# Dilated attention on Trainium2: the two key blocks of dilation 1 folded into one tile of scores

## The chip, the cores and the metric

The kernel runs on one core of one Trainium2 chip. Its time is the device time of one launch in microseconds, and the median of several runs is compared. The engines have the names of the profile: PE (TensorE matmuls), PEld (its weight loads), DVE (VectorE), ACT (ScalarE), POOL (GpSimd) and SP (SyncE, which here only issues DMAs).

## The reference

The kernel computes one step of a hybrid decoder layer: in every layer, an HGRN2 recurrence and a dilated sliding-window attention run beside each other on a prompt of 2048 positions and on eight sample requests, followed by an output projection, a ConvFFN and a per-layer input gate. Only the prompt's attention is touched here. It has 8 heads of 64 channels and three dilations, whose partial results are merged by their maxima and sums:

```python
DILATIONS = ((128, 1), (512, 4), (2048, 16))      # window, dilation
dist = qi - kj + ATTN_BLOCK                       # qi: 128 queries, kj: 256 keys (previous block, own block)
for window, dil in DILATIONS:
    n_back = window // dil                        # 128 for each
    ...
    valid = (dist >= 0) & (dist <= n_back) & (blk * ATTN_BLOCK - ATTN_BLOCK + kj >= 0)
    s = jnp.einsum('brnqhc,brnkhc->brnhqk', qs, kb)
    s = jnp.where(valid[None, None, :, None], s, NEG_INF)
    m = s.max(axis=-1)
    p = jnp.exp(s - m[..., None])
    l = p.sum(axis=-1)
    acc = jnp.einsum('brnhqk,brnkhc->brnqhc', p, vb)
    parts.append((from_sub(m), from_sub(l), from_sub(acc)))
w = jnp.exp(ms - ms.max(axis=0, keepdims=True))   # combine_dilations
return (w[..., None] * accs).sum(0) / (w * ls).sum(0)[..., None]
```

In dilation 1 each query reads 129 keys: its own position and the 128 before it. In a block of 128 queries, a query at place i of the block reads own keys at places 0 to i and the previous block's keys at places i to 127. So at each place there is exactly one key that counts, own or previous, except at place i itself, where both count (distances 0 and 128).

## The kernel before

**Stages.** The first stage, up to about 837 us, holds the input projection and most of the HGRN2 recurrence. The attention stage follows, to about 1213 us, and then the trunk (output projection, ConvFFN, gate), whose matmuls fill PE to the end. In the attention stage the prompt's attention is interleaved with side work: the last unit of the recurrence, the attention of the samples (its keys and values arrive as 32 DMAs of 1 MB into tiles `skt`), and the samples' recurrence.

**Order.** On PE the order of instructions is the order of a table set by hand. On DVE, ACT and POOL a scheduler places them by an estimate of when their inputs come. The DMAs of this stage are issued mostly by SP, in the order of its queue.

**Blocks and units.** Heads are taken in four pairs, p = 0 to 3. A pair has two kinds of blocks of 128 queries. With `di == 0`, dilations 4 and 16 are done together: the queries are every fourth position of a chunk of 512, the keys all positions of their residue up to the chunk's end (1 to 4 tiles of 128 keys), and a key that both dilations read counts twice, by adding log 2 to its score. With `di == 1`, dilation 1, there are 16 blocks with two key blocks each, the previous and the own one (the first block only has its own). A unit is one block with both heads, or with one head where it has 3 or 4 key tiles. There are 160 units: 40 to a head pair, the last 16 of them dilation 1 for pairs 0 to 2. In pair 3 both kinds alternate.

**Steps.** Step x of the loop `for x in range(n + 19)` issues, for unit x, `scores`: four matmuls into a bank `S` of PSUM (keys split in a high part `kH` and a low part `kL`, L797 and L798), a DVE instruction for each head that adds the mask, writes the result `P` to SBUF and takes the minimum (L802; scores are held negated), and ACT's exponential with its sum (L803). At odd x, two older units (x-3 and x-2) are `turned`: PE transposes `P` into a bank `PT` (L810), and the result is copied to SBUF as `pt`, for three of four units by DVE and for the fourth by ACT (L812). Then the units x-7 and x-6 are summed: `weighted` multiplies `pt` with the values into a bank `acc` (L822). Four blocks, a group, share one `acc`; after the fourth, ACT copies it to SBUF as `o` (L872). There are 32 groups.

**Merge and staging.** After each dilation-1 group `merge` (L728 to L761) combines it with the same queries' other group: statistics go out and come back by DMA, DVE and POOL make the weights, ACT one exponential, and coefficients go out and come back. For the next head pair, `stage` loads queries and keys by DMA, and `stack` writes them to `qS`, `kH` and `kL` (L695 is ACT's part), in four pieces around the end of the pair before.

**Banks.** In PSUM, `S`, `acc` and `PT` have two banks each; the rest is for the side work.

Of the kernel before, what the change touches and what calls it, by code (L numbers as in the profile page):

```python
# [28 lines left out]
BIG = 1e30  # L29
# [18 lines left out]
def hymba_step_kernel(ctx: ExitStack, tc: tile.TileContext, I: dict, O: dict):  # L48
# [624 lines left out]
    def attn_phase(spare, rest):  # L673
# [29 lines left out]
        qS = rp.tile([128, 2, SEQ], F32R, name="qS")  # L703
        kH = rp.tile([128, 2, 4, 512], F32R, name="kH")
        kL = rp.tile([128, 2, 4, 512], F32R, name="kL")
        mask = wk.tile([128, 768], F32, name="mask", bufs=1)
        SP.dma_start(mask, I["amask"])
        stack(0, *first)
        yield
        vals = {}  # L710
# [52 lines left out]
        class Block:  # L763


            def __init__(self, p, di, c, r):
                self.p, self.di, self.c, self.r = p, di, c, r
                self.pt = {}
                if di == 0:
                    self.q = lambda hh: qS[:, hh, 512 * c + r:512 * c + 512:4]  # L770
                    self.nk = c + 1
                    self.k = lambda t, hh: t[:, hh, r, :128 * c + 128]
                    self.v = [(n, r) for n in range(c + 1)]
                else:
                    b = 4 * c + r
                    self.q = lambda hh: qS[:, hh, 128 * b:128 * b + 128]
                    self.nk = 2 if b else 1
                    self.k = lambda t, hh: t[:, hh].rearrange("p r (n i) -> p n r i", i=32)[:, b + 1 - self.nk:b + 1]
                    self.v = [(x // 4, x % 4) for x in range(b + 1 - self.nk, b + 1)]
                hi = (512, 768)[di]  # L780
                self.mask = mask[:, hi - 128 * self.nk:hi]

        class Unit:
# [5 lines left out]
            def scores(self, both):  # L789
                bl = self.block  # L790
                bl.both, bl.st = both, both[:, 1]
                st = bl.st
                w = 128 * bl.nk
                s = pS.tile([128, 512], F32, name="S")
                self.pe = wk.tile([128, 512], F32, name="P", bufs=6)
                for i, hh in enumerate(self.heads):
                    PE.matmul(s[:, w * i:w * i + w], lhsT=bl.q(hh), rhs=bl.k(kH, hh), start=True, stop=False)  # L797
                    PE.matmul(s[:, w * i:w * i + w], lhsT=bl.q(hh), rhs=bl.k(kL, hh), start=False, stop=True)  # L798
                for i, hh in enumerate(self.heads):
                    pe = self.pe[:, w * i:w * i + w]  # L800
                    mn = st[:, bl.r, hh, 1:2]
                    V.tensor_tensor_reduce(pe, s[:, w * i:w * i + w], bl.mask, 1.0, 3e38, ALU.add, ALU.min, mn)  # L802
                    A.activation(pe, pe, AF.Exp, bias=mn, scale=-1.0, accum_out=st[:, bl.r, hh, 0:1])  # L803

            def turned(self, on_act):
                nk = self.block.nk
                n = nk * len(self.heads)
                pt = pT.tile([128, 4, 128], F32, name="PT")
                for i in range(n):
                    PE.transpose(pt[:, i], self.pe[:, 128 * i:128 * i + 128], ident)  # L810
                out = wk.tile([128, 4, 128], F32, name="pt", bufs=8)
                (A.copy if on_act else V.tensor_copy)(out[:, :n], pt[:, :n])  # L812
                for i, hh in enumerate(self.heads):
                    self.block.pt[hh] = out[:, nk * i:nk * i + nk]
# [790 lines left out]
    for x in in_phase(1, *args, plv, po):  # L1605
# [5 lines left out]
        else:  # L1611
# [3 lines left out]
    pool = pools(attn_st)  # L1615
    pps = pool("s_ps", 1, space=PSUM)
    rest += (pool("a_d", 2), pool("a_r", 1), pool("a_w", 3), pool("a_s", 3),
             pool("a_pS", 2, space=PSUM), pool("a_pA", 2, space=PSUM), pool("a_pT", 2, space=PSUM))
    step(main, 1)

    def others():
# [43 lines left out]
def _constants():  # L1665

    f = np.float32
    c = {}
    c["ident"] = np.eye(128, dtype=f)
    inv = (500000.0 ** (-np.arange(8) * 0.125)).astype(f)  # L1670
    pos = np.zeros((17, 128), f)
    pos[:16] = np.arange(SEQ, dtype=f).reshape(16, 128)
    pos[16, :NS] = (16384 + np.arange(NS) % 4).astype(f)
    ang = (pos[:, :, None] * inv).astype(np.float64)
    cos, sin = np.cos(ang).astype(f), np.sin(ang).astype(f)
    c["rope"] = np.ascontiguousarray(np.concatenate([cos, cos, -sin, sin], -1).transpose(1, 0, 2))
    i = np.arange(128)


    dist = i[:, None] - i[None, :] + 128 * np.arange(3, -1, -1)[:, None, None]  # L1680
    count = ((dist >= 0) & (dist <= 128)) + ((dist >= 0) & (dist % 4 == 0)).astype(int)
    order = 4 * (i % 32) + i // 32
    keep = np.stack([order[None, :] >= i[:, None], order[None, :] <= i[:, None]]).astype(int)
    count = np.concatenate([count, keep]).transpose(1, 0, 2).reshape(128, 768)
    c["amask"] = np.where(count == 0, BIG, np.where(count == 2, -np.log(2.0), 0.0)).astype(f)
    m = np.zeros((128, 9, 2, 64), f)
    for li, h in enumerate(LEVELS):
        for a, n in enumerate((h, 2 * h, 2 * h)):
            right = i[(i // n) % 2 == 1]
            part = ((i[:, None] // (2 * n)) == (right[None, :] // (2 * n))) & ((i[:, None] // n) % 2 == 0)  # L1690
            if a:
                part &= (i[:, None] // h) % 2 == 2 - a
            m[:, 3 * li + a] = part[:, None]
    m = m.reshape(128, 9, 128)
    c["lvl_mask"] = m
    j = np.arange(NS)
    m = np.zeros((NS, 2, NS), f)
    for li, h in enumerate((2, 1)):
        m[:, li] = (((j[:, None] // (2 * h)) == (j[None, :] // (2 * h))) & ((j[:, None] // h) % 2 == 0)
                    & ((j[None, :] // h) % 2 == 1))  # L1700
    c["lvl_mask_s"] = m
    c["bmask"] = (j[:, None] // 4 == np.arange(8)[None, :]).astype(f)

    t = np.arange(128) % 4
    w = (np.arange(128)[None, :] * 4 + np.arange(4)[:, None]).reshape(-1)
    dist = 512 + t[:, None] - w[None, :]
    mw = (dist <= 128).astype(f) + ((dist % 4 == 0) & (dist <= 512)).astype(f)
    md = (np.repeat(np.arange(4), 128)[None, :] == t[:, None]).astype(f)
    mult = np.concatenate([mw, md], 1)
    logs = lambda n: np.where(n > 0, -np.log(np.maximum(n, 1.0, dtype=np.float64)), BIG).astype(f)  # L1710
    c["s_neg"] = logs(mult)
    mn = np.zeros((128, 2, NS), f)
    for g in range(2):
        for r in range(128):
            b, tt = 4 * g + r // 32, r % 4
            mn[r, g, 4 * b:4 * b + tt] = 1.0
            mn[r, g, 4 * b + tt] = 3.0
    c["s_negn"] = logs(mn)
    head = (np.arange(128) % 32) // 4
    c["s_hmask"] = (head[:, None] == np.arange(512)[None, :] // 64).astype(f)  # L1720
    bt = (np.arange(128) // 32) * 4 + t
    c["s_sel"] = (bt[:, None] == np.arange(16)[None, :]).astype(f)
    return c
# [75 lines left out]
```

## Time and profile before

| what | value |
|---|---|
| median of 3 runs | 3017.25 us (3016.31 to 3018.32) |
| the profiled execution's own time | 3014.84 us |
| its span in the profile | 3013.0 us |
| mean granted clock of PE | 0.988 of full speed |
| instructions in the profile | 52001 |
| bytes moved by DMA | 664.08 MB, 220 GB/s in the mean |

The span is the time from the first to the last recorded instruction; the run's time is 1.8 us longer. In rows of windows, each engine has its busy microseconds and the count of its instructions, followed by the clock that PE was granted, the share of time in which the 16 DMA engines were busy in the mean (it can read above 1), and GB/s. In rows of groups, the part behind the bar is busy time and the mean of one in ns, then the idle time of the engine ahead of them and what ended it. In rows of the chain, the first number is the place in the span and the second the share of the chain that the step takes. A row of the timeline has start, duration, engine, line and operation, and in square brackets the idle time ahead with what ended it; matmuls overlap in the pipeline, so the time from start to start tells how fast they go.

### The profile page before, as it was taken

The numbers are of one execution on the slowest core, as the hardware profiler recorded it, in microseconds if no ns is written. First come the engines' busy times: TensorE is split into PE (matmuls) and PEld (weight loads), VectorE is DVE, ScalarE is ACT, GpSimd is POOL, SyncE is SP. The second block draws the span as 40 slices with busy tenths as digits, with TensorE's granted clock in tenths as the row PEclk, the third lists the DMA queues.
The fourth block names the chain that finished last, engine by engine and source line by source line (L and its number), as shares of the span: only waits on it lengthen the run. The fifth ranks groups of instructions, "written<-read, shape, count | busy, mean of one in ns | idle before, by whom it ended". The sixth has DMA issues, their size and how long they took to land.

```text
span 3013.0 us, 52001 instructions
## 1 busy us (share of the span) xinstructions
PE 2926.5 (97%) x18639; PEld 2738.0 (91%) x18639; DVE 2191.6 (73%) x4761; ACT 1304.5 (43%) x2824; POOL 667.9 (22%) x780
## 2 busy tenths in 40 slices
PE   8999999999978989999999999999999999999998
PEld 8977789987767667999999999999999999999997
DVE  7666868884466557568988889766769777777777
ACT  5333423231156665334444444544444544444443
POOL 1443222221134553102443431000001000000000
PEclk9999999999989999999999999999999999999999
DMA  5898533342248996766666568677778777778873
GB/s 174 311 337 309 198 103 110 104 134 95 91 115 243 303 246 194 260 225 222 227 209 194 191 198 300 231 250 252 245 231 311 242 245 244 257 248 290 272 274 131
DMA packets 328579, 664.08 MB, mean 220 GB/s; under 512 B 46400, under 2 KB 114112, under 8 KB 326528
## 3 DMA queue, kind: packets, MB, share of 16 engines
q1 hardware_dynamic: 291472, 472.65, 48.4%
q0 software_dynamic: 33264, 121.13, 12.6%
q10 hardware_dynamic: 3584, 66.98, 6.1%
q8 instruction: 147, 2.41, 0.3%
q14 instruction: 112, 0.92, 0.1%
HBM read 513.69 MB, written 213.92 MB: 241 GB/s over the span
## 4 chain that ended last, share of the span: by engine, by line
PE 72%; issue 9%; DVE 7%; DMA 7%; ACT 2%; POOL 2%; SPq 1%; DVEq 0%; POOLq 0%; ACTq 0%
PE mm L142 16%; PE mm L144 16%; PE mm L143 16%; PE mm L346 2%; PE mm L344 2%; PE mm L345 2%; PE lv L484 2%; PE acc L822 2%; PE S L797 1%; PE PT L810 1%; PE S L798 1%; DMA draw<-in_w_down_dram 1%; DMA xr<-in_xT_dram 1%; DVE h L1291 1%; DMA wd_d<-dw 1%
## 5 line engine op out<-in xcount | busy, mean ns | idle before, releaser
L143 PE MATMUL mm<-w 128*128 128x348 f32 (+3 forms) x3636 | 1166.1, 321 | 1.1 <-DVE w L1435 0.7
L142 PE MATMUL mm<-w 128*128 128x348 f32 (+3 forms) x3508 | 1109.7, 323 | 15.2 <-ACT s L1233 5.8
L144 PE MATMUL mm<-w 128*128 128x348 f32 (+3 forms) x3508 | 1117.4, 321 | 1.3 <-DVE w L181 1.3
L143 PEld LDWEIGHTS mm<-w 128*128 128x128 f32 x3636 | 684.3, 188 | 3.8 <-DVE w L1067 1.8
L142 PEld LDWEIGHTS mm<-w 128*128 128x128 f32 x3508 | 656.5, 188 | 23.6 <-ACT s L1233 8.5
L144 PEld LDWEIGHTS mm<-w 128*128 128x128 f32 x3508 | 659.0, 188 | 2.6 <-DVE w L181 1.8
L181 DVE TENSOR_TENSOR w<-raw,w 128x512 fp32r<-128x512 f32 x586 | 421.9, 725 | 170.3 <-ACT w L180 165.3
L180 ACT CAST w<-raw 128x512 fp32r<-128x512 f32 x586 | 360.6, 621 | 402.8 <-PE mm L144 293.1
L1275 POOL DMA_DIRECT2D w<-wd_d x231 | 123.8, 536 | 906.2 <-PE mm L144 800.6
L1291 DVE TENSOR_TENSOR h<-h,mm 128x348 f32<-128x348 f32 (+1 forms) x504 | 248.4, 509 | 45.9 <-PE mm L144 44.4
L803 ACT ACTIVATE P<-P,st 128x256 f32<-128x256 f32 (+3 forms) x256 | 134.1, 526 | 87.5 <-DVE st L802 85.9
L802 DVE CUSTOM_DVE_ANT_0 P<-S,mask 128x256 f32<-128x256 f32 (+3 forms) x256 | 105.0, 449 | 73.1 <-PE S L798 50.1
L1233 ACT COPY s<-mm 128x348 f32<-128x348 f32 (+1 forms) x198 | 87.9, 444 | 158.1 <-PE mm L144 157.8
L345 PE MATMUL mm<-wl,xh 128*128 128x512 f32 x352 | 140.7, 400 | 1.1 <-DVE wl L267 1.1
L344 PE MATMUL mm<-wh,xh 128*128 128x512 f32 x352 | 140.6, 403 | 0.0
L346 PE MATMUL mm<-wh,xl 128*128 128x512 f32 x352 | 140.3, 399 | 0.0
L142 PE MATMUL mm<-xh,wh 128*128 128x384 f32 (+2 forms) x384 | 125.7, 332 | 8.6 <-ACT xh L242 5.1
L143 PE MATMUL mm<-xl,wh 128*128 128x384 f32 (+2 forms) x384 | 126.9, 333 | 0.8 <-DVE xl L243 0.8
L144 PE MATMUL mm<-xh,wl 128*128 128x384 f32 (+2 forms) x384 | 125.5, 330 | 1.5 <-DVE wl L267 1.4
L267 DVE TENSOR_TENSOR wl<-wraw,wh 128x512 fp32r<-128x512 f32 x104 | 86.3, 851 | 34.0 <-POOL wh L148 28.9
L181 DVE TENSOR_TENSOR dw<-draw,dw 128x512 fp32r<-128x512 f32 x77 | 69.4, 909 | 55.8 <-ACT dw L180 55.0
L797 PE MATMUL S<-kH,qS 128*128 128x256 f32 (+3 forms) x256 | 97.7, 396 | 8.2 <-DVE st L802 7.3
(348 smaller groups left out, 5155.0 us busy)
## 6 DMA issues: line engine op xcount, KB each, us to landing
w<-wd_d POOLq DMA_DIRECT2D x231, 512.0 KB, 5.6
wd_d<-dw SPq DMA_DIRECT2D x77, 512.0 KB
out_sk_dram<-in_cache_k_dram ACTq DMA_DIRECT2D x56, 584.0 KB
out_sv_dram<-in_cache_v_dram ACTq DMA_DIRECT2D x56, 584.0 KB
raw<-in_w_gate_dram SPq DMA_DIRECT2D x110, 256.0 KB
raw<-in_w_up_dram SPq DMA_DIRECT2D x110, 256.0 KB
wraw<-in_w_in_dram SPq DMA_DIRECT2D x104, 256.0 KB
raw<-w_gate_d SPq DMA_DIRECT2D x88, 256.0 KB
```

The source lines that it names most:

```text
L142: PE.matmul(ps, lhsT=wh, rhs=xh, start=first, stop=False, skip_group_check=read)
L143: PE.matmul(ps, lhsT=wh, rhs=xl, start=False, stop=False, skip_group_check=read)
L144: PE.matmul(ps, lhsT=wl, rhs=xh, start=False, stop=last, skip_group_check=read)
L180: A.copy(w[:, 0], raw)
L181: V.tensor_sub(w[:, 1], raw, f32(w[:, 0]))
L344: PE.matmul(ps, lhsT=xh[k][:, js], rhs=wh, start=k == 0, stop=False)
L345: PE.matmul(ps, lhsT=xh[k][:, js], rhs=wl, start=False, stop=False)
L346: PE.matmul(ps, lhsT=xl[k][:, js], rhs=wh, start=False, stop=k == NK - 1)
L797: PE.matmul(s[:, w * i:w * i + w], lhsT=bl.q(hh), rhs=bl.k(kH, hh), start=True, stop=False)
L803: A.activation(pe, pe, AF.Exp, bias=mn, scale=-1.0, accum_out=st[:, bl.r, hh, 0:1])
L1275: G.dma_start(t, wd_d[p][n - 1])
L1291: V.tensor_add(o, o, acc[m][:, :H])
```

## The change

In every dilation-1 block with two key blocks, 60 of the 64, the two tiles of scores are folded into one. A predicated copy on DVE, with a 0/1 mask `ahead`, writes the previous block's scores over the own block's at the places whose own key is ahead of the query, in PSUM. What remains is one tile of 128 columns for each head in place of 256: one DVE minimum over both heads, exponentials of 128 columns straight out of PSUM, and one transpose for each head in place of two. The sums still need the probabilities as two tiles, one for each key block. So in place of the copy of the transposed tiles to SBUF, DVE multiplies each of the two transposed tiles by two 0/1 masks (`sides`), one for the previous and one for the own block, and writes four tiles. All 60 products are on DVE; before, a quarter of the copies was on ACT.

The key at distance 128, whose place now belongs to the own block, moves to the blocks of `di == 0` (it is read there as the key 32 steps back in the residue), where its count rises by one, so log 3 appears beside log 2 in the mask. The mask grows from 768 to 1024 columns, and one DVE instruction casts `ahead` to bytes. The first block of each pair is not folded. The banks of PSUM are given out anew: `S` gets three, `acc` one, `PT` keeps two.

```diff
-        mask = wk.tile([128, 768], F32, name="mask", bufs=1)
+        mask = wk.tile([128, 1024], F32, name="mask", bufs=1)
         SP.dma_start(mask, I["amask"])
+        ahead = wk.tile([128, 128], U8, name="ahead", bufs=1)
+        V.tensor_copy(ahead, mask[:, 640:768])
+        sides = mask[:, 768:].rearrange("p (o n t) -> p o n t", o=1, n=2).to_broadcast([128, 2, 2, 128])
...
-                hi = (512, 768)[di]
+                self.folded = di == 1 and self.nk == 2
+                hi = (512, 640)[di]
...
+                if bl.folded:
+                    two = s.rearrange("p (h n t) -> p h n t", h=2, n=2)
+                    V.copy_predicated(two[:, :, 1], ahead.rearrange("p (o t) -> p o t", o=1).to_broadcast([128, 2, 128]),
+                                      two[:, :, 0])
+                    V.tensor_reduce(st[:, bl.r, :, 1], two[:, :, 1], axis=mybir.AxisListType.X, op=ALU.min)
+                    for hh in range(2):
+                        A.activation(self.pe[:, 128 * hh:128 * hh + 128], two[:, hh, 1], AF.Exp,
+                                     bias=st[:, bl.r, hh, 1:2], scale=-1.0, accum_out=st[:, bl.r, hh, 0:1])
+                    return
...
+                if self.block.folded:
+                    pt = pT.tile([128, 4, 128], F32, name="PT")
+                    for hh in range(2):
+                        PE.transpose(pt[:, hh], self.pe[:, 128 * hh:128 * hh + 128], ident)
+                    out = wk.tile([128, 4, 128], F32, name="pt", bufs=8)
+                    V.tensor_mul(out.rearrange("p (h n) t -> p h n t", h=2),
+                                 pt[:, :2].rearrange("p h (o t) -> p h o t", o=1).to_broadcast([128, 2, 2, 128]), sides)
+                    for hh in range(2):
+                        self.block.pt[hh] = out[:, 2 * hh:2 * hh + 2]
+                    return
...
-             pool("a_pS", 2, space=PSUM), pool("a_pA", 2, space=PSUM), pool("a_pT", 2, space=PSUM))
+             pool("a_pS", 3, space=PSUM), pool("a_pA", 1, space=PSUM), pool("a_pT", 2, space=PSUM))
...
-    count = ((dist >= 0) & (dist <= 128)) + ((dist >= 0) & (dist % 4 == 0)).astype(int)
+    count = ((dist >= 0) & (dist <= 128)) + ((dist >= 0) & (dist % 4 == 0)).astype(int) + (dist == 32)
...
-    c["amask"] = np.where(count == 0, BIG, np.where(count == 2, -np.log(2.0), 0.0)).astype(f)
+    add = np.where(count == 0, BIG, -np.log(np.maximum(count, 1.0)))
+    c["amask"] = np.concatenate([add, 1 - own, 1 - own.T, own.T], 1).astype(f)
```

The instruction counts move as follows. PE makes 448 transposes in place of 568; its matmuls and their order stay, but for six matmuls of the trunk. DVE gets 60 predicated copies, 60 minima, 60 products and the cast, and loses 120 masked minima (152 with 256 columns before, 32 after) and 44 copies. ACT makes 120 exponentials of 128 columns in place of 120 of 256, and 16 copies fewer. POOL and SP issue the same instructions in a partly different order. Since three lines of code were added ahead of `merge` and more within `scores` and `turned`, L797 is L801 after the change, L803 is L809 in folded units, L810 is L824, L812 is L826, L822 is L845 and L872 is L895.

PE in head pair 1, at the last unit of the first folded group and what follows. The rows show a unit's scores, the transposes of two older units, the sums of two blocks, the first of which opens a group's `acc`, and matmuls of the samples' attention (`s2`). Before:

```order
L797 MATMUL S_10701<-kH_8624,qS_8623 128x256
L798 MATMUL S_10701<-kL_8625,qS_8623 128x256
L810 MATMUL PT_10711<-c_ident_64,P_10628 128x128 x4
L810 MATMUL PT_10718<-c_ident_64,P_10638 128x128 x4
L822 MATMUL acc_10725<-pt_10597,v_10391 64x128 x2
L822 MATMUL acc_10725<-pt_10604,v_10391 64x128 x4
L965 MATMUL s2_10461<-skt_10738,sPT_10372 32x512 x4
```

After:

```order
L801 MATMUL S_10667<-kH_8624,qS_8623 128x256
L802 MATMUL S_10667<-kL_8625,qS_8623 128x256
L824 MATMUL PT_10677<-c_ident_64,P_10598 128x128 x2
L824 MATMUL PT_10682<-c_ident_64,P_10608 128x128 x2
L845 MATMUL acc_10687<-pt_10569,v_10363 64x128 x2
L845 MATMUL acc_10687<-pt_10574,v_10363 64x128 x4
L988 MATMUL s2_10433<-skt_10700,sPT_10344 32x512 x4
```

The order is the same; each turned unit has two transposes for four. The group's `acc` is now the only bank for sums, so its first matmul needs the copy of the group before.

DVE at the same place: scores of the unit, then the older units' transposed tiles, then a merge's instruction (`mn`). Before:

```order
L802 ISA P_10702,st_10626<-S_10701,mask_8626 128x256
L802 ISA st_10626 128x1
L802 ISA P_10702,st_10626<-S_10701,mask_8626 128x256
L802 ISA st_10626 128x1
L812 COPY pt_10716<-PT_10711 128x512
L812 COPY pt_10723<-PT_10718 128x512
L736 TENSOR_REDUCE mn_10984<-st_10626 128x8
```

After:

```order
L805 COPY_PREDICATED S_10644<-ahead_8628,S_10644 128x2x128
L805 COPY_PREDICATED S_10667<-ahead_8628,S_10667 128x2x128
L807 TENSOR_REDUCE st_10596<-S_10644 128x2
L826 TENSOR_TENSOR pt_10680<-PT_10677,mask_8626 128x512
L826 TENSOR_TENSOR pt_10685<-PT_10682,mask_8626 128x512
L807 TENSOR_REDUCE st_10596<-S_10667 128x2
L745 RECIPROCAL mn_10809<-mn_10809 128x8
L739 TENSOR_REDUCE mn_10930<-st_10596 128x8
```

The two predicated copies of a pair of units come first, and the second unit's minimum now stands behind both products.

ACT a little later, up to the copy of the group's sums to SBUF. Before:

```order
L803 ACTIVATE P_10746,st_10744<-P_10746,st_10744 128x256
L738 ACTIVATE w_10985<-w_10985 128x16
L803 ACTIVATE P_10746,st_10744<-P_10746,st_10744 128x256
L803 ACTIVATE P_10756,st_10744<-P_10756,st_10744 128x256
L812 COPY pt_10777<-PT_10772 128x512
L803 ACTIVATE P_10756,st_10744<-P_10756,st_10744 128x256
L872 COPY o1_10787<-acc_10725 128x512
```

After:

```order
L695 CAST kH_8624<-stage_10587 128x4x128
L809 ACTIVATE P_10708,st_10706<-S_10707,st_10706 128x128 x2
L741 ACTIVATE w_10931<-w_10931 128x16
L809 ACTIVATE P_10718,st_10706<-S_10717,st_10706 128x128 x2
L895 COPY o1_10745<-acc_10687 128x512
```

The copy of the sums keeps its place behind the exponentials of its pair of units; the copy of transposed tiles ahead of it is gone.

More of the change, by code (lines that the diff above doesn't have):

```diff
@@ L1680, in _constants @@
     dist = i[:, None] - i[None, :] + 128 * np.arange(3, -1, -1)[:, None, None]
[L1681 removed]
+    count = ((dist >= 0) & (dist <= 128)) + ((dist >= 0) & (dist % 4 == 0)).astype(int) + (dist == 32)
     order = 4 * (i % 32) + i // 32
[L1683 to L1685 removed]
+    own = (order[None, :] <= i[:, None]).astype(int)
+    count = np.concatenate([count, own[None]]).transpose(1, 0, 2).reshape(128, 640)
+    add = np.where(count == 0, BIG, -np.log(np.maximum(count, 1.0)))
+    c["amask"] = np.concatenate([add, 1 - own, 1 - own.T, own.T], 1).astype(f)
     m = np.zeros((128, 9, 2, 64), f)
```

## The prediction

> **What bounds the kernel now.** I read the page first, then busy time by stretch, then the chain of waits, then the groups by form.
>
> ```profile
> span 3013.0 us, 52001 instructions
> PE 2926.5 (97%) x18639; PEld 2738.0 (91%) x18639; DVE 2191.6 (73%) x4761; ACT 1304.5 (43%) x2824; POOL 667.9 (22%) x780
> core 0: us, PE busy (x) PEld busy (x) DVE busy (x) ACT busy (x) POOL busy (x), PEclk, DMA share, GB/s
> 837.00:1213.00 376.00, 339.07 (x2913) 267.63 (x2913) 246.79 (x869) 237.08 (x698) 170.24 (x205) 0.94 0.79 219
> 899.00:940.00 41.00, 34.02 (x312) 29.03 (x310) 32.63 (x114) 30.66 (x99) 23.55 (x31) 0.92 0.62 192
> 990.00:1027.00 37.00, 35.13 (x325) 24.70 (x317) 22.31 (x87) 26.79 (x81) 30.98 (x38) 0.95 1.03 318
> 1083.00:1120.00 37.00, 33.46 (x319) 23.79 (x315) 20.93 (x85) 26.75 (x76) 27.18 (x34) 0.95 0.88 228
> 1120.00:1204.00 84.00, 80.49 (x741) 67.67 (x737) 63.50 (x241) 50.39 (x169) 32.81 (x47) 0.98 0.69 193
> ```
>
> Overall the kernel is bound by PE. The attention stage, 837 to 1213 us, is the only one that the change touches; PE is busy for 339 of its 376 us. The next four rows hold the 60 units that will be folded, 15 each: dilation 1 of head pairs 0, 1 and 2, and all of pair 3. They differ. In the first, PE idles 7 us and DVE is busy 80%. In the second PE (35 of 37), POOL (31) and the DMA engines (share 1.03) are all nearly full. In the third PE idles 3.5 us, in the fourth 3.5 of 84. The chain says what fills them:
>
> ```profile
> 1008.09 0.87 PE PT L810 x8
> 1008.97 1.02 PE acc L822 x16
> 1009.99 0.99 PE s L965 x8
> 1093.04 9.12 DMA stage<-qT_d
> 1103.06 6.47 DMA stage<-qT_d
> 932.14 2.09 ACT kH L695 x2
> 934.23 1.49 ACT P L803 x6
> 841.43 5.70 DMA mask<-in_amask_dram
> ```
>
> The first three rows are one pair of dilation-1 units on PE: eight transposes, the sums, the side work. But in the third stretch the chain runs through two stage loads for the next head pair (15.6 us), and in the first through ACT. There a shorter PE stream shortens little.
>
> **The change part by part.**
>
> *Transposes.* 60 units make two instead of four: 120 x 0.87/8 = 0.109 us, 13.1 us of PE, 3.3 us per stretch. Where PE sets the pace it is all gain. I take all of it in the fourth stretch (-3.3), half in the second, since POOL and DMA are the next to be late there (-1.6), a third in the first (-1.1, cover: DVE and ACT) and a third in the third (-1.1, cover: the stage loads). Sum -7.1; ends -13.1 and 0.
>
> *DVE.* The nearest rows:
>
> ```profile
> L802 DVE CUSTOM_DVE_ANT_0 P<-S,mask 128x256 f32<-128x256 f32 x152 | 56.8, 420 | 29.5 <-PE S L798 18.8 <-issue 2.7 <-ACT P L803 2.6
> L812 DVE COPY pt<-PT 128x512 f32<-128x512 f32 x80 | 53.2, 683 | 2.4 <-PE PT L810 2.4
> L496 DVE COPY_PREDICATED at<-msk,lv 128x128 f32<-128x128 uint8 x252 | 82.0, 342 | 7.3 <-PE lv L484 6.1
> L942 DVE TENSOR_REDUCE sl<-sP 128x1 f32<-128x1056 f32 x2 | 2.5, 1248 | 0.8 <-ACT sP L941 0.8
> L736 DVE TENSOR_REDUCE mn<-st 128x8 f32<-128x16 f32 x16 | 2.7, 171 | 0.4 <-DMA st<-stat_d 0.4
> L575 DVE TENSOR_TENSOR hg<-ms,hg 128x512 f32<-128x512 f32 x14 | 9.3, 685 | 0.0
> ```
>
> Gone per unit: two masked minima (2 x 0.420) and 44 of 60 turned copies (0.683; the other 16 were ACT's), 1.34 us. New: a predicated copy of 256 elements, a minimum of 256, and a product of 512 out of PSUM (0.685, the same form as L575). The minimum lies on the line through L736 and L942: 0.171 + 240 x (1.248 - 0.171)/1040 = 0.42. The predicated copy has no row of its size or with its output in PSUM; it lies between L496's 0.342 (half the elements) and twice that, 0.684. L802 streams as many elements from PSUM in 0.420, so I take 0.43. New sum 1.54, or +0.2 per unit, +12 us of DVE (ends +6.4 and +27). DVE has 15 us idle in the second stretch and 16 in the third, which hides 3 us there; in the first it has 8, and DVE is late there already. I put +2 on the path; ends 0 and +8.
>
> *ACT.* An exponential falls from 256 elements in SBUF to 128 in PSUM, and 16 copies leave:
>
> ```profile
> L803 ACT ACTIVATE P<-P,st 128x256 f32<-128x256 f32 x152 | 75.9, 502 | 29.2 <-DVE st L802 28.3 <-ACT P L803 0.9
> L803 ACT ACTIVATE P<-P,st 128x128 f32<-128x128 f32 x40 | 15.7, 394 | 17.3 <-DVE st L802 17.0
> L812 ACT COPY pt<-PT 128x512 f32<-128x512 f32 x28 | 16.0, 570 | 6.0 <-PE PT L810 5.9
> L872 ACT COPY o<-acc 128x512 f32<-128x512 f32 x32 | 26.5, 829 | 3.7 <-DVE o L760 1.8 <-PE acc L822 1.6
> ```
>
> 120 x 0.108 + 16 x 0.57 = 22 us of ACT. PE hides it except where ACT is on the chain, in the first stretch: -1; ends -3 and 0.
>
> *One bank for the sums.* A group's sums may now start only when ACT has copied the group before (L872). What waits is PE's first matmul of the group, and behind it in PE's order the next scores and transposes. In ACT's new order the copy still follows the exponentials of its pair, at places behind kH casts and a merge's exponential too. Before, a second bank hid that. Reading each of the 31 hand-overs off the timeline's rows of L872 and L822, five copies end later than the next group starts, by 0.1, 0.6, 0.6, 2.0 and 2.6 us. One of them, its next group starting at 972.53 and its copy ending at 974.52, and the last, whose copy stands inside 48 loads that ran on unhindered:
>
> ```profile
> 972.53 0.64 PEld L822 LDWEIGHTS acc<-pt,v 128*64 128x64 f32 x12 [0.17 <-issue]
> 973.44 1.08 ACT L872 COPY o<-acc 128x512 f32<-128x512 f32 x1
> 1206.43 4.26 PEld L822 LDWEIGHTS acc<-pt,v 128*64 128x64 f32 x48 [0.17 <-issue]
> 1209.62 1.11 ACT L872 COPY o<-acc 128x512 f32<-128x512 f32 x1
> ```
>
> Sum 5.8, less what PE then need not wait for elsewhere: +5. Ends 0 and 31 x 0.83 = +26 (every copy wholly in the open).
>
> *Third score bank.* It can take away only waits of the scores for DVE:
>
> ```profile
> PE S L797 <- DVE st L802: 7.3, 5, 4.4
> ```
>
> The 4.4 is the start, where DVE waits for the mask; the rest, 2.9, is the most. The folded scores are also held longer, through ACT's exponentials: -1.5; ends -2.9 and +2.
>
> *Mask.* 1024 columns for 768 on a load that is on the chain: a third of 5.70 is 1.9; part of it is latency, so +1; ends 0 and 1.9. The cast of `ahead` is one DVE instruction while PE waits for the first unit anyway: 0. POOL's and SP's work is the same and reordered; I put 0 on it.
>
> Sum: -7.1 + 2 - 1 + 5 - 1.5 + 1 = -1.6. The profiled execution took 3014.84 us (span 3013.0 and 1.8 around it); the median of the runs is 3017.25, 2.4 above. 3014.84 - 1.6 + 2.4 = 3015.6. About 0.2%, 6 us, is what a measurement of this kernel can tell from no change.
>
> **The rivals.**
>
> *The transposes' time arrives.* If the sum bank's lateness falls into waits that PE has anyway, and lighter ACT and the third bank let PE run ahead, three quarters of 13.1 stay, with -1 and -1.5 beside them, and +2 and +1 against: -9.3, about 3008. For it: 80.5 of 84 us busy in the fourth stretch, 35 of 37 in the second. Against: 15.6 us of stage loads on the chain of the third.
>
> *The sum bank decides: slower.* Each dilation-1 pair now runs predicated copies, minimum, two products, second minimum on DVE, so the pair's last exponentials come later, and ACT's copy behind them. If the copy starts more than about 1 us after its last sum at most hand-overs, PE stands still at each. At 28 of them, 0.57 us (half of 0.83 and the late start): +16 in place of +5, so 3015.6 + 11, about 3026. For it: in the first, second and third stretch ACT is busy 72 to 75%, and one copy already ended 2 us late. Against: 26 of 31 copies came in time. The Trainium skill (Perfetto Trace Analysis, Matmuls) says that independent matmul groups should rotate through different PSUM banks so that the evacuation of one overlaps the next group's matmuls. By that rule the change gives up the overlap, and the sum would be nearer to +26 for this term; the five of 31 speak for a small part of it.
>
> *The clock.* Where PE stalls, it comes back slow:
>
> ```profile
> 1022.00:1038.00 16.00, 15.74 (x110) 11.93 (x109) 5.26 (x24) 9.84 (x34) 8.51 (x11) 0.79 1.09 278
> 1034.07 0.40 PE L798 MATMUL S<-kL,qS 128*128 128x128 f32 x1
> 1034.30 0.40 PE L797 MATMUL S<-kH,qS 128*128 128x128 f32 x1
> 1007.22 0.28 PE L797 MATMUL S<-kH,qS 128*128 128x256 f32 x1
> 1007.34 0.28 PE L798 MATMUL S<-kL,qS 128*128 128x256 f32 x1
> 982.64 0.63 PE L797 MATMUL S<-kH,qS 128*128 128x512 f32 x1 [0.62 <-DVE st L802]
> 999.26 0.39 PE L797 MATMUL S<-kH,qS 128*128 128x256 f32 x1 [0.24 <-DVE st L802]
> 974.00:990.00 16.00, 14.49 (x123) 1.00 1.05 332
> 990.00:1006.00 16.00, 15.76 (x158) 1.00 1.06 367
> ```
>
> From start to start, scores of 128 columns took 0.23 us at 1034, and those of 256 columns took 0.12 at 1007, before the stall at 1022. The granted clock was 0.79 in the first row's window, so 0.21 x 16 = 3.4 us of full speed were lost. If new short pauses make three more such spells, +10 on the forecast: 3026. Against: the pauses at 982.64 and 999.26, of 0.62 and 0.24 us, left the clock at 1.00 in their windows (the last two rows: PE busy, then the clock). The Trainium skill (TensorE: Matmul & The Clock Gate, HAM oscillation) describes such spells after PE idles; the rows show the spell, not how long an idle time starts it.
>
> **How the numbers follow.** Forecast 0.45; time arrives 0.30; sum bank 0.17; clock 0.08. The forecast's own range, 3011 to 3022 (transposes -10 to -4, bank +2 to +8), lies within 0.2%, so same 0.45, faster 0.30, slower 0.25. The range 3005 to 3028 takes in 3008 and 3026 with the open prices around them (the predicated copy at 0.684, a spell of slow clock more or less) and leaves under 2 in 10.
>
> **What would show it.** Right: 448 transposes for 568; stretches two and four shorter by 1.5 to 3 us, one and three by about 1; a new wait of the sums' first matmul for L872's copy, 3 to 8 us in all; DVE busier by some 12 us. Predicated copy at 0.38 to 0.50 us. Wrong: a second stretch of 33 us or less (the time arrived), waits for the copy over 12 us, or more windows with a clock under 0.9 than before. What would make the total wrong is the order on SP and POOL, which I priced at nothing: a stage load issued some us later at a head pair's end moves PE by as much.

## The result: slower by 0.51%

The changed kernel takes 3033.43 us in the median of 5 runs (3027.78 to 3037.36). Against the kernel before, 3017.25 us, the ratio is 1.0051, interval 1.0038 to 1.0064: about 16 us slower. The prediction was 3015.6 us, its range ended at 3028. The profiled execution took 3030.45 us.

The page after, its span and busy times:

```profile
span 3028.7 us, 51673 instructions
PE 2920.7 (96%) x18519; PEld 2732.3 (90%) x18519; DVE 2204.0 (73%) x4658; ACT 1281.0 (42%) x2808; POOL 674.4 (22%) x780
```

PE works less, DVE 12 us more and ACT 23 us less, as forecast; the span grows by 15.7 us. All of it lies in the attention stage, taken here from the first scores to the first matmul of the trunk (behind it the trunk takes 1800 us in both). Windows of the stage with PE alone (length, PE busy and its instructions, granted clock, DMA share, GB/s), before and after:

```profile
837.59:1212.59 375.00, 338.66 (x2911) 0.94 0.79 219
```

```profile
836.66:1229.15 392.49, 335.14 (x2792) 0.91 0.78 211
```

The stage is 17.5 us longer. PE's idle time there goes from 36.3 to 57.4 us, 21 more. PE's busy time should fall by the 120 transposes, 13.1 us, and falls by 3.5: the rest of its work ran 9.6 us slower, at a clock of 0.91 for 0.94. What the idle time is, the view of waits on PE tells (total, times, longest; 836 to 1236 us). Its rows for ACT and for the side loads, before:

```profile
PE s L928 <- DMA skt<-in_kT_d_dram: 5.1, 2, 2.8
PE PT L810 <- ACT pt L812: 2.0, 3, 1.4
PE PT L810 <- ACT P L803: 0.9, 2, 0.7
```

After:

```profile
PE PT L824 <- ACT P L809: 10.1, 9, 3.6
PE acc L845 <- ACT o L895: 9.4, 3, 5.3
PE s L951 <- DMA skt<-in_kT_d_dram: 6.1, 3, 2.7
PE S L801 <- ACT P L809: 5.6, 3, 3.1
```

PE now waits 25 us for ACT, for exponentials and for the copy of the sums, in 15 waits, where ACT's exponentials and copies had held it for 3. ACT has less to do than before. In part it is late because it waits itself, for POOL's part of the merges and for stage loads. These waits of ACT (860 to 1236 us) before:

```profile
ACT w L738 <- POOL w L737: 6.2, 4, 3.0
ACT kH L695 <- DMA stage<-kT_d: 6.1, 2, 5.1
```

After:

```profile
ACT w L741 <- POOL w L740: 10.6, 5, 5.4
ACT kH L695 <- DMA stage<-kT_d: 7.9, 3, 3.7
```

So ACT waited before the change too, and only 6 us less; what is new is how much of it reaches PE. Two places in the timeline after, ACT and then PE:

```profile
1125.39 1.11 ACT L695 CAST kH<-stage 128x512 fp32r<-128x512 f32 x1 [3.72 <-DMA stage<-kT_d]
1128.26 0.50 PE L801 MATMUL S<-kH,qS 128*128 128x128 f32 x1 [3.12 <-ACT P L809]
1222.75 0.22 ACT L741 ACTIVATE w<-w 128x16 f32<-128x16 f32 x1 [5.44 <-POOL w L740]
1223.96 0.48 PE L845 MATMUL acc<-pt,v 128*64 128x128 f32 x2 [5.25 <-ACT o L895]
```

At 1125 ACT stands at the cast of the next keys, which come by DMA; the exponentials behind it hold a bank of scores, and PE stops. At 1223 ACT stands at a merge's exponential, and the copy of the only sums bank is behind it. These two are among the five longest waits, which make 17.8 of the 25 us. Of the other three, one stands behind a cast that waits for a stage load (3.6 us), one behind a copy of the sums that waits for DVE's addition at the end of a merge (3.5), and one behind a merge's exponential and then late minima of DVE (2.3). The other ten waits are of 1.7 us and less.

The new instructions cost what was put on them. Groups by form, after:

```profile
L805 DVE COPY_PREDICATED S<-ahead,S 128x256 f32<-128x256 uint8 x60 | 25.0, 426 | 17.5 <-PE S L802 15.5 <-ACT o L895 0.9 <-issue 0.2
L807 DVE TENSOR_REDUCE st<-S 128x2 f32<-128x256 f32 x60 | 24.8, 416 | 0.1
L826 DVE TENSOR_TENSOR pt<-PT,mask 128x512 f32<-128x512 f32 x60 | 39.2, 682 | 4.2 <-PE PT L824 4.2
L809 ACT ACTIVATE P<-S,st 128x128 f32<-128x128 f32 x120 | 42.7, 366 | 34.4 <-DVE st L807 31.1 <-PE S L802 0.8 <-DVE rs_t L104 0.8
```

### The profile page after: what moved, and what is told of

It is laid out like the page before. It is cut to its first block, busy times and chain, and to the rows that moved or that the text cites. A ratio compares the mean times of both kernels' runs of the same rounds, so it can differ in the third digit from the quotient of the medians.

```text
span 3028.7 us, 51673 instructions
## 1 busy us (share of the span) xinstructions
PE 2920.7 (96%) x18519; PEld 2732.3 (90%) x18519; DVE 2204.0 (73%) x4658; ACT 1281.0 (42%) x2808; POOL 674.4 (22%) x780
## 4 chain that ended last, share of the span: by engine, by line
PE 42%; issue 15%; DVE 4%; DMA 2%; POOL 2%; ACT 1%; SPq 0%; POOLq 0%; DVEq 0%; ACTq 0%
PE mm L142 13%; PE mm L143 12%; PE mm L144 12%; POOL w L1298 1%; PE acc L845 1%; DVE h L1314 1%; PE S L801 1%; DVE w L181 1%; PE S L802 0%; PE PT L833 0%; PE mm L129 0%; DMA skt<-in_kT_d_dram 0%; DMA st<-stat_d 0%; PE s L650 0%; DMA coef_d<-wt 0%
## 5 line engine op out<-in xcount | busy, mean ns | idle before, releaser
L801 PE MATMUL S<-kH,qS 128*128 128x256 f32 (+3 forms) x256 | 98.8, 400 | 11.3 <-ACT P L809 5.6
L801 PEld LDWEIGHTS S<-kH,qS 128*128 128x128 f32 x256 | 66.6, 260 | 44.9 <-issue 24.8
L816 ACT ACTIVATE P<-P,st 128x128 f32<-128x128 f32 (+3 forms) x136 | 74.2, 546 | 76.8 <-DVE st L815 66.8
```

## The experiments

Theories ahead of the runs: A, the single sums bank; B, score banks held until ACT has read them; C, the fold's own chain on DVE and ACT; D, the loads set the pace. Two came up on the way: E, a moved order of the DMAs on SP meets full DMA engines; F, DVE stands at the end of merges. Ratios are against the kernel before, measured beside each run, with 95% intervals.

**Banks and transposes apart.** `fold_222`: the changed kernel with banks 2, 2, 2. `banks_312`: the kernel before with 3, 1, 2 (the same line, the other way round).

```diff
-             pool("a_pS", 3, space=PSUM), pool("a_pA", 1, space=PSUM), pool("a_pT", 2, space=PSUM))
+             pool("a_pS", 2, space=PSUM), pool("a_pA", 2, space=PSUM), pool("a_pT", 2, space=PSUM))
```

> The fold as changed, with the banks as before: two for the scores, two for the sums. Theory A (one bank for the sums makes it slower: in the changed kernel PE stood 0.6, 3.5 and 5.3 us for ACT's copy of the sums): the loss goes, and the kernel takes 3008 to 3016 us, at or below before. Theory B (the scores' banks are held until ACT's exponentials have read them, and ACT stands behind casts that wait for stage loads): with two banks for the scores instead of three the scores wait more, so 3030 to 3045 us. Theory C (the fold itself, by later exponentials and products on DVE, whatever the banks): 3027 to 3035, as changed.

Measured 3036.17 us, 1.0054 (1.0035 to 1.0073). Giving the sums their second bank back at the price of the third score bank wins nothing. Theory A as the cause of the whole falls, unless the score banks eat up what the sums win; `sbuf_222` below takes both away.

```profile
PE S L801 <- ACT P L809: 22.6, 15, 8.5
PE s L951 <- DMA skt<-in_kT_d_dram: 7.8, 3, 4.0
```

With two score banks PE waits 22.6 us for ACT to release one, with three it was 5.6.

> The kernel before with three banks for the scores, one for the sums, and nothing folded. Theory A (one bank for the sums): slower by 6 to 16 us, 3023 to 3033. Theories B and C: the sums' bank costs only what the prediction's five late copies say, 6 us less what the third score bank gives: 3015 to 3022.

Measured 3024.0 us, 1.0021 (1.0007 to 1.0034): 7 us by the medians, at the low end of theory A's range, but the interval (2 to 10 us) reaches into the other one. Here the sums do wait (the profiled execution is 4.5 us above the median):

```profile
PE acc L822 <- ACT o L872: 11.1, 5, 3.8
```

`half_turn`: the kernel before, with two of four transposes in the 60 units.

```diff
+                if self.block.di == 1 and nk == 2:
+                    pt = pT.tile([128, 4, 128], F32, name="PT")
+                    for hh in range(2):
+                        PE.transpose(pt[:, hh], self.pe[:, 256 * hh:256 * hh + 128], ident)
+                    out = wk.tile([128, 4, 128], F32, name="pt", bufs=8)
+                    (A.copy if on_act else V.tensor_copy)(
+                        out.rearrange("p (h n) t -> p h n t", h=2),
+                        pt[:, :2].rearrange("p h (o t) -> p h o t", o=1).to_broadcast([128, 2, 2, 128]))
...
```

> The kernel before with banks as before, where each of the 60 units makes two transposes in place of four and the copy to SBUF writes each of them twice. The other key block's probabilities are left out, so its output is not attention; it is there for the time of the 120 transposes alone, everything else on DVE and ACT being as before. If the transposes' time arrives: 13 us less, 3002 to 3006. If the stage loads and the side work's loads bound the stretches (theory D), 3010 to 3017. If the waits that a faster PE runs into even lower the clock, above 3017.

Measured 3020.93 us, 1.0005 (0.9994 to 1.0017). 13 us of PE's work are gone, and nothing is won (-2 to +5 us). The stage of its profiled execution:

```profile
836.62:1215.83 379.21, 330.01 (x2792) 0.92 0.78 217
```

Against the kernel before PE is busy 8.7 us less and idle 12.9 us more (49.2). The transposes' time turned into waits, with a lower clock beside them. From first scores to first scores in the timeline, the dilation-1 blocks of pair 1 took 33.4 us for 36.2 and those of pair 2 31.0 for 37.2. It was lost elsewhere: the dilation-1 blocks of pair 0 took 42.9 for 40.8, the other blocks of pair 2 59.6 for 56.3, and units 124 to 158 (pair 3) 73.5 for 70.4.

A rival stays open here. The edit also makes the scheduler place other instructions anew: with names compared in the two traces, at least 67 of SP's 1709 DMAs stand in another place of its queue, and the orders on DVE, ACT and POOL differ too. `before_mask` below moves at least 20 of SP's DMAs and is 7 us slower. So the run shows that the transposes' time does not arrive together with the moved orders; what it would bring in the old orders was not run.

**Who frees the score bank, and the predicated copy.** `fold_sbuf`: as changed, but DVE writes the folded scores to SBUF. `sbuf_222`: the same with banks 2, 2, 2.

```diff
+        zero = wk.tile([128, 128], F32, name="zero", bufs=1)
+        G.memset(zero, 0.0)
...
-                    V.tensor_reduce(st[:, bl.r, :, 1], two[:, :, 1], axis=mybir.AxisListType.X, op=ALU.min)
                     for hh in range(2):
-                        A.activation(self.pe[:, 128 * hh:128 * hh + 128], two[:, hh, 1], AF.Exp,
-                                     bias=st[:, bl.r, hh, 1:2], scale=-1.0, accum_out=st[:, bl.r, hh, 0:1])
+                        pe = self.pe[:, 128 * hh:128 * hh + 128]
+                        V.tensor_tensor_reduce(pe, two[:, hh, 1], zero, 1.0, 3e38, ALU.add, ALU.min,
+                                               st[:, bl.r, hh, 1:2])
+                        A.activation(pe, pe, AF.Exp,
+                                     bias=st[:, bl.r, hh, 1:2], scale=-1.0, accum_out=st[:, bl.r, hh, 0:1])
```

> The changed kernel, but the folded scores are written to SBUF by DVE with their minimum (one instruction for each head, adding a tile of zeros), and ACT's exponential works there, so that DVE and not ACT frees the bank of the scores. Banks 3, 1, 2 as changed. Theory B (banks held until ACT): PE's waits of the scores for ACT (3.1 and 2.3 us at 1128 and 1162) go, with the slow clock behind them, 3018 to 3026. Theories A and C: 0.2 us more of DVE for each unit and nothing gained, 3030 to 3040.

Measured 3036.42 us, 1.0056 (1.0036 to 1.0076): theory B alone falls.

> The changed kernel with both of its banks' waits taken away at once: DVE writes the folded scores to SBUF, so that DVE frees their bank, and the banks are 2, 2, 2 as before, so that the sums have two. If holding the scores for ACT (23 us of waits in the run with two score banks) and the single sums bank (9.4 us in the changed kernel) make the loss between them: 3015 to 3024. If it is DVE's and ACT's lateness that shows at whatever PE needs next: 3028 to 3038, and the waits move to the transposes.

Measured 3029.69 us, 1.0033 (1.0021 to 1.0045). With neither kind of bank in the way, the waits moved to the loads and the transposes; the banks between them are worth about 4 of the 16 us, and the intervals overlap. So who frees a bank does not explain most of the loss. Among PE's largest waits are now these:

```profile
PE s L955 <- DMA skt<-in_kT_d_dram: 14.6, 6, 5.0
PE PT L828 <- ACT P L813: 7.2, 8, 1.7
```

`after_nocp`: the changed kernel without the line `V.copy_predicated(...)`.

> The changed kernel without its 60 predicated copies: the own block's scores alone go into the minimum and the exponentials, so the previous block's keys are left out wrongly. All else is as changed, banks too. Theory C: DVE has 26 us less and the exponentials come 0.4 to 0.9 us earlier in each pair of units, so a good part of the loss goes, 3018 to 3026. If the copies are hidden and the loss is the sums' bank and the loads: 3028 to 3034.

Measured 3028.74 us, 1.0038 (1.0023 to 1.0053), at the low end of the second expectation: 25 us of DVE taken away are worth about 5, with intervals that overlap. Most of the copies' time is hidden.

**DVE's order.** `after_dve`, `before_dve`: the order of the code for DVE too.

```diff
-    with tc.manual_schedule(engines={mybir.EngineType.PE}):
+    with tc.manual_schedule(engines={mybir.EngineType.PE, mybir.EngineType.DVE}):
```

> The changed kernel with DVE's order in the attention stage also fixed to the order of the code, in place of the scheduler's: now each unit's predicated copy is followed at once by its minimum, and both minima of a pair stand ahead of the pair's two products (in the scheduler's order the second minimum stood behind them). If the late minima make the exponentials and ACT's copy of the sums late (theory C, place in DVE's order): 3016 to 3025. If the loss is elsewhere, or DVE now waits ahead of other work: 3030 to 3045.

> The kernel before with DVE's order in the attention stage fixed to the order of the code in the same way: the control for the run above. Its masked minima stood ahead of the copies already, so nothing is to be won there: 3015 to 3025 by every theory. What it moves away from 3017 is the price of the order as such.

Measured 3103.12 (1.028, 1.0263 to 1.0296) and 3082.56 us (1.0208, 1.0194 to 1.0223). All expectations missed: DVE in the order of the code costs the kernel before 65 us. In the trace of `before_dve` DVE's waits for POOL at the merges (L742 and L760) are 83.5 us, where they were 17.7. The two runs still differ by 20.6 us with the minima ahead of the products, which speaks against the late second minimum as the cause; with so many other waits beside it, it is no proof.

**The loads.** In the `light` kernels each of the 32 side loads brings 256 KB:

```diff
-                    SP.dma_start(kt, I[src][4 * g:4 * g + 4, :, p].rearrange("b d j -> d b j"))
+                    SP.dma_start(kt[:, 0], I[src][4 * g, :, p])
...
-                        PE.matmul(ps[32 * bi:32 * bi + 32], lhsT=qb[:, 4 * g + bi, p], rhs=kt[:, bi],
+                        PE.matmul(ps[32 * bi:32 * bi + 32], lhsT=qb[:, 4 * g + bi, p], rhs=kt[:, 0],
```

(and the same for the values). Three quarters of the samples' keys and values are left out.

> The kernel before, where each of the 32 loads of the samples' keys and values (skt) brings 256 KB in place of 1 MB, and all four matmuls of a step read that one block; three quarters of the samples' keys and values are left out. The same number of DMAs, matmuls and waits. Theory D (from 926 to 1102 us the DMA engines are full, and these loads and the stage loads set the pace): faster by 6 to 20 us, 2997 to 3011. If the DMA engines were full without being the bound: 3013 to 3018.

> Two transposes for four in the 60 units, as in the run before with the full loads (half the keys' probabilities left out), now with the loads of 256 KB. Theory D: without full DMA engines the transposes' time arrives, 8 to 13 us below the kernel before with light loads. If it is the engines in order (DVE, ACT) that eat the time and not the DMAs: within 3 us of it, as with full loads.

> The changed kernel with the loads of 256 KB (three quarters of the samples' keys and values left out). Theory D, that the changed kernel loses because its stalls meet late loads: no slower than the kernel before with light loads, or up to 8 us faster. Theory C (the fold's own chain, predicated copy, minimum, exponential, product, copy of the sums, costs 16 us whatever the loads): 10 to 20 us slower than the kernel before with light loads.

Measured 3005.58 us (0.9959, 0.9944 to 0.9974), 3010.41 (0.9974, 0.9964 to 0.9984) and 3015.73 (0.9996, 0.9987 to 1.0006). The loads are worth 12 us before and 18 after, so by the medians theory D is right for about 6 of the 16. But the transposes' time does not arrive without full DMA engines either: `light_half` is 5 us above `light_before` and misses both of its expectations. The fold still costs 10, the low end of theory C. Here too the scheduler moved SP's DMAs, at least 39 from the kernel before to `light_before`, and from that at least 31 to `light_half` and 41 to `light_after`; their part was not separated.

**The mask.** `before_mask`: the kernel before with the mask's load of 1024 columns and a cast of 128 columns. `before_cast`: the cast alone. `light_mask`: `before_mask` with light loads.

```diff
-        mask = wk.tile([128, 768], F32, name="mask", bufs=1)
+        mask = wk.tile([128, 1024], F32, name="mask", bufs=1)
         SP.dma_start(mask, I["amask"])
+        ahead = wk.tile([128, 128], U8, name="ahead", bufs=1)
+        V.tensor_copy(ahead, mask[:, 768:896])
...
```

> The kernel before with the mask's load grown from 768 to 1024 columns and the cast of one DVE instruction to bytes, nothing else: this part of the change alone. By the prediction's term +1 us, 3017 to 3020. If a small edit that makes the scheduler place DVE's, ACT's and POOL's instructions anew can by itself cost what the changed kernel lost, 3025 or more.

> The kernel before with only the cast of 128 mask columns to bytes added; the mask's load keeps its 768 columns, and no instruction changes its place on any engine or queue. Theory E: nothing, 3015 to 3020. If the cast ahead of the first minima, on the chain of the first unit, were the cost: 3022 to 3026.

> The kernel before with the mask of 1024 columns and the cast, and with the samples' loads of 256 KB (three quarters of their keys and values left out). If the wider mask's 7 us come from loads that arrive late (theory E: the moved order on SP meets full DMA engines): within 3 us of the kernel before with light loads, 3003 to 3009. If they come from the orders on DVE and ACT or from the mask's own load: 3010 to 3014.

Measured 3024.28 us (1.0022, 1.0011 to 1.0034), 3019.55 (1.0003, 0.9994 to 1.0012) and 3006.16 (0.9958, 0.9942 to 0.9973). The wider mask alone makes the kernel 7 us slower, between its two expectations, and with light loads 0.6. The load itself is not what costs: DVE's wait for it goes from 4.9 to 5.5 us. With it the scheduler, which places instructions by an estimate of when inputs come, moves at least 20 of SP's 1709 DMAs in the trace, and instructions on DVE, ACT and POOL; with the cast alone it moves none. One such place on SP, where a side load falls behind a write that waits for a merge (names without their numbers; - before, + with the wider mask):

```
  DMA skt<-in_v_w_dram 128x4x512
- DMA skt<-in_v_w_dram 128x4x512
- DMA cf<-coef02_d 64x1024 x2
  DMA mix_d<-o1 128x512
+ DMA cf<-coef02_d 64x1024 x2
+ DMA skt<-in_v_w_dram 128x4x512
```

The waits of `before_mask` on PE (its profiled execution is 7.6 us above its median, so this is a bad case of it):

```profile
PE s L930 <- DMA skt<-in_kT_d_dram: 15.1, 6, 4.7
```

5.1 us before, 15.1 here: the loads that PE waits for come later. Whether a moved order or the 128 KB more is what delays them was not separated.

**What stays with light loads.** `light_sbuf222`: `sbuf_222` with light loads. `light_split`: the changed kernel with light loads and, for the product, the copies of `half_turn`.

> The fold with scores written to SBUF by DVE and banks 2, 2, 2, with the samples' loads of 256 KB (three quarters of their keys and values left out). If the fold's 10 us under light loads come from the score banks that ACT holds and the one sums bank: within 4 us of the kernel before with light loads, 3003 to 3009. If they come from DVE's longer chain as such: 3012 to 3018.

> The changed kernel where the product with the 0/1 masks is a plain copy of each transposed tile into both places, by ACT for one unit in four as before, with the samples' loads of 256 KB (three quarters of their keys and values, and the masks of the two sides, are left out). If the fold's 10 us under light loads come from all products being on DVE: 3006 to 3010. If the products are hidden: 3012 to 3018, as the changed kernel with light loads.

Measured 3013.84 us (0.9983, 0.9971 to 0.9994) and 3018.83 (1.0, 0.9987 to 1.0013). Neither the banks (2 us by the medians) nor the products are the 10 us. The traces of the light kernels show what grew. DVE's waits in `light_before`, `light_half` and `light_after`:

```profile
DVE o L760 <- POOL o L758: 8.0, 6, 3.2
```

```profile
DVE o L760 <- POOL o L758: 19.6, 8, 5.0
```

```profile
DVE o L763 <- POOL o L761: 22.2, 8, 4.9
```

This is the addition that ends a merge. One of them in the timeline of `light_half`, on POOL, DVE and PE:

```profile
1064.07 2.50 POOL L758 TENSOR_TENSOR o<-o,cf 128x512 f32<-128x512 f32 x2 [5.26 <-DMA cf<-coef_d]
1066.60 0.69 DVE L760 TENSOR_TENSOR o<-o,o 128x512 f32<-128x512 f32 x1 [5.02 <-POOL o L758]
1067.82 0.63 PE L797 MATMUL S<-kH,qS 128*128 128x512 f32 x1 [2.90 <-DVE st L802]
```

POOL waits for the coefficients' way out and back, DVE for POOL, and PE for the minima behind DVE's addition. That way has no fixed length: from ACT's copy of the weights `wt` to POOL's first product, the four merges of pair 1 took 9.0 us in the mean in `light_before`, 12.0 in `light_half` and 12.4 in `light_after`, mostly because SP issues the reads of the coefficients later (3.9, 6.5 and 6.8 us behind the copy). `light_after_g` and `light_before_g` put that addition on POOL for all head pairs:

```diff
-            (G if p == 3 else V).tensor_add(parts[1], parts[1], parts[0])
+            G.tensor_add(parts[1], parts[1], parts[0])
```

> The changed kernel with the samples' loads of 256 KB (three quarters of their keys and values left out), where the addition that ends a merge runs on POOL for all head pairs, in place of DVE for pairs 0 to 2. DVE then waits no more for POOL's products, which wait for the coefficients' way out and back by DMA. Theory F (the faster steps of PE meet that wait of fixed length, and DVE's scores stand behind it): 6 to 12 us less than the changed kernel with light loads, 3004 to 3010. If those waits of DVE are hidden: 3012 to 3018.

> The kernel before with the same light loads and the same move of the addition to POOL: the control. DVE waits only 8 us there for POOL's products, so by theory F 0 to 5 us less than 3005.6. A gain here as large as in the changed kernel would mean that the move as such, not the wait that the fold lengthens, makes it.

Measured 3004.41 us (0.9951, 0.9936 to 0.9966) and 3000.99 (0.9938, 0.9916 to 0.9961). The fold gains 11 us by it, the control 5 (14 and 6 by the ratios); of the 10 us between them 3.4 are left. So with light loads about two thirds of what the fold costs is DVE standing in its order at the end of merges. The same move with full loads was not run. There these waits of DVE are 8.1 us before and 6.7 after, so by the traces this path carries little of the loss of the changed kernel itself; one of PE's five longest waits (3.5 us) does stand behind such an addition.

## Why the prediction was wrong

- *What bounds.* "Overall the kernel is bound by PE", and busy shares of 35 of 37 and 80.5 of 84 us were read as stretches that PE sets. `half_turn` does not bear that out: with 13.1 us less of PE's work, in an order that the scheduler moved as well, the time stays. A busy share of 95% leaves out that PE's clock gives way (0.94 to 0.92 there) and that PE then waits for loads and merges, which it reaches earlier.
- *Transposes, -7.1.* This is the step that failed first: the gain measured is nothing (-2 to +5 us, moved orders included), where 7.1 were counted. The cover that it named (POOL, DMA, stage loads) was there in part, but it was counted within each stretch. In `half_turn` two stretches of dilation 1 do win 2.8 and 6.3 us, and more than that is lost in the others.
- *Mask +1, and "POOL's and SP's work is the same and reordered; I put 0 on it".* This is the second step that failed. The mask's part alone measured 7, of which light loads leave 0.6; the load itself kept to its term (DVE waits 0.6 us longer for it in `before_mask`, 0.3 in the changed kernel). What was put at nothing is most likely what was wrong, the orders that move and what they meet on the DMA engines, though the 128 KB more were not separated from them. In the changed kernel at least 45 of SP's DMAs stand in another place. The last part of the prediction named the order on SP as what would make the total wrong; it gave it no price.
- *One bank for the sums, +5, and the third score bank, -1.5.* Right in kind: 7 in `banks_312` for the two, where 3.5 was forecast and the interval (2 to 10) does not exclude it. In the changed kernel three of 31 hand-overs waited, 9.4 us. They are not "most hand-overs", as the rival had it: its time (3026) came nearest, with the clock rival's, but by luck, since its mechanism did not decide: `fold_222` with two banks for the sums is as slow, and `sbuf_222` wins back about 4.
- *DVE +12 us, ACT -22 us of busy time.* 12.4 and 23.5 were measured; 0.43, 0.42 and 0.685 us were 0.426, 0.416 and 0.682. What was wrong is what lies on the path: ACT's lighter load was counted as a gain of 1, but exponentials that read PSUM tie PE's banks to ACT's queue (5.6 us of waits with three score banks, 22.6 with two), and ACT's queue waits for DMAs and for POOL. Rows of before showed ACT waiting (6.1 us for stage loads, 6.2 for the merges) and 2.9 us of PE's waits for ACT; what they could not show is scores held for ACT, since DVE freed their banks. "Ends -2.9 and +2" was too narrow.
- *What was to show it.* Of the stretches, none came as forecast. From first scores to first scores in the timeline they took 2.0 and 3.3 us more (the first and second), 5.1 less (the third, where PE had stalled 3.5 us; a stall of 3.1 us now stands behind its end) and 8.7 more (the fourth). Of 16 us windows from 846 on, 9 had a clock under 0.9 for 7 before, which the prediction had named as a sign against it.
- *The clock rival.* Its price of +10 is about what was measured, 9.6 us of slower running. But it did not come from short pauses alone: it came with 21 us more of idle time, which that rival did not price.

What stays open: the terms are not shown to add up. The mask's 7 us and the 10 us with light loads make 17 beside the 16 measured, but the second was explained in kernels with light loads. With full loads, that ACT's waits for the stage loads and the merge carry the loss is read from one trace. The run that takes ACT out of the release of the score banks and gives the sums a second bank, `sbuf_222`, wins back about 4 us, so most of the cause is not shown. Nearly every run also moved the scheduler's orders (only `before_cast` moved none), and no run held them still; how much of the loss is the fold and how much the orders is not known.

## What to carry to other kernels

Before a saving on the busiest engine is counted, take it away by a kernel that leaves the work out: here 13 us less of PE's work did not shorten the kernel. Then compare the orders on the other engines and on the DMA queue: when a scheduler places the instructions, even the smallest edit of a load moves others, and a run of that edit by itself gives its price (7 us here). Where engines run in order, look at what stands behind each instruction that waits for a DMA. Whether a release of buffers is better given to an engine whose queue waits less is not shown: `fold_sbuf` gave it to DVE and won nothing.

## What the runs showed of the hardware

The predicated copy of 256 elements from PSUM into PSUM took 426 ns, about as much as the masked minimum of as many (420); with half the elements, out of PSUM into SBUF, it took 342 in the kernel before. An exponential of 128 columns out of PSUM took 366 ns, and 394 out of SBUF.
